# A float32 decoder layer on one Trainium2 core: branch products ahead of the gates, gate products by 2x2 blocks with seven products, merge through device memory

## The chip, the cores and the metric

The kernel runs on one core of a Trainium2 chip. A core has a matrix engine (TensorE, PE in the rows), two engines for element-wise work (VectorE, DVE, and ScalarE, ACT), a third one (GpSimd, POOL), and queues for transfers between device memory and the on-chip memory, issued here from SyncE (SP), ACT and POOL. Each engine works off its own instructions in the order of the program and waits by semaphores for the others. The metric is the time of one launch on the device in microseconds (us); lower is better.

## The reference

One decoder layer over x of 512 tokens by 2048 features, in float32:

```
proj = x @ W_in        # HGRN2 [q|f|i|g], attention [q|k|v], gates [gate_A|gate_B]
y_A  = hgrn2(q, f, i, g) @ W_A          # 1024 x 2048
y_B  = window_attention(q, k, v) @ W_B  # 1024 x 2048
x    = LN(alpha*x + (sigmoid(gate_A)*y_A + sigmoid(gate_B)*y_B) @ W_out)
x    = LN(alpha*x + relu(x @ W1)**2 @ W2)   # W1 2048 x 8192
```

What the change concerns is the middle: the two gates, each a product of x (512 x 2048) with 2048 columns of W_in, the two branch products y_A and y_B, and their sum weighted by the gates.

## The kernel before

Matrices lie on chip with features on the 128 partitions and the 512 tokens along the free dimension. Float32 precision is made from three products in a rounded 32-bit format: every operand is split into a high part (`hi`, made by ACT, line 84) and a low part (`lo = src - hi`, made by DVE, line 85), and `mm3` (lines 113 to 116) issues hi·hi, hi·lo and lo·hi for each pair. So each weight tile of 128x1024 costs a transfer on the SP queue, one ACT and one DVE instruction, and feeds 24 matmuls of 128x512 (moving size 512) or 24 of 128x256.

The stages run one after the other: attention, then HGRN2 by pairs of heads (`hg_pair`), then gates and branches, then `@ W_out` with the first LN, then the first product of the feed-forward part (FFN-1), its second product (FFN-2) and the second LN. The last thing each HGRN2 head does is `hg_out` (lines 480 to 508): a chain PE (L483, state updates) to DVE (L486, L488) to PE (L493, L495, the head's output) to ACT (L499, squares) to DVE (L500 to L502, an inverse square root by Newton steps and a product) to PE (L506, transposes) to DVE (L508). All its PSUM tiles come from the one bank `sc`, so two heads' chains go one after the other.

Gates and branches (lines 551 to 582) run over c = 0..7, 256 columns each: gate B (96 matmuls of 128x512), sigmoid on ACT, gate A (96), sigmoid, branch y_B (48), product with the gate on DVE, branch y_A (48), product on DVE and sum on POOL into `mix`, which stays on chip. At the end `mix` is split into `bh`, `bl`, the operands of `@ W_out`. The operands of the branches, `ath`, `atl` (from attention) and `oh`, `ol` (from HGRN2), are split at c = 0.

FFN-1 (lines 700 to 822) has 32 groups of 256 columns. The first four are plain (`head`: 96 matmuls of 128x512 a group). The other 28 cut the group's product into 2x2 blocks (two halves of the 2048 features, two halves of the 256 columns, two halves of the 512 tokens) and make it with seven block products in place of eight: each is 24 matmuls of 128x256 (`prod1`), and the sums of blocks that it needs are made on DVE, of the weights in each group (`tt`, 128x1024) and of x once ahead of the groups (`room`, `xq`: q6, q7 and q3, and q5 overwritten). In a group, product A takes the weights of block b11 as loaded, B needs the DVE sums, C a difference. Part of group g (`tail`: two products) is done inside group g+1.

The kernel is laid out by a scheduler that simulates the time of each instruction and sets each engine's order from it; what stands earlier in the program has the better priority. Buffers of weights: `raw` 3, `wh` 3, `wl` 2; `mz` 4 of 128x2048; PSUM `mm` 4 banks, `tp` 3, `sc` 1.

Of the kernel before, what the change touches and what calls it, by code (L numbers as in the profile page):

```python
# [10 lines left out]
F32 = mybir.dt.float32  # L11
F32R = mybir.dt.float32r
# [5 lines left out]
P = 128  # L18
# [34 lines left out]
def layer(ctx, tc, xt, xn, win, wa, wb, wo1, wo2, w1, w2, cst, vec, lnv, out):  # L53
# [56 lines left out]
    def wview(w, c):  # L110
        return w[0][:].rearrange("p (k c) -> p k c", c=c), w[1][:].rearrange("p (k c) -> p k c", c=c)
# [432 lines left out]
    pr_ctx = ExitStack()  # L544
    pb = pr_ctx.enter_context(tc.tile_pool(name="pb", bufs=1))
    ath = pb.tile([P, 8, T], F32R, name="ath")
    atl = pb.tile([P, 8, T], F32R, name="atl")
    oh = pb.tile([P, 8, T], F32R, name="oh")
    ol = pb.tile([P, 8, T], F32R, name="ol")
    mix = []  # L550
    for c in range(8):
        pgb = proj_fm([win[G_GB + c, q] for q in range(4)], bh, bl)
        sb = []
        for m in range(2):
            s = pb.tile([P, T], F32, tag="sb", bufs=2, name=nm("sb"))
            ACT.activation(s[:], pgb[m][:], AF.Sigmoid)
            sb.append(s)
        pga = proj_fm([win[G_GA + c, q] for q in range(4)], bh, bl)
        sa = []
        for m in range(2):  # L560
            s = pb.tile([P, T], F32, tag="sa", bufs=2, name=nm("sa"))
            ACT.activation(s[:], pga[m][:], AF.Sigmoid)
            sa.append(s)
        if c == 0:
            for i in range(8):
                split(ath[:, i, :], atl[:, i, :], att[i // 4][:, i % 4, :])
        yb = proj_fm([wb[c, q] for q in range(2)], ath, atl)
        if c == 0:
            for i in range(8):
                split(oh[:, i, :], ol[:, i, :], oT[i // 4][:, i % 4, :])  # L570
        if c % 2 == 0:
            mt = pm.tile([P, 4, T], F32, tag="mz", bufs=4, name=nm("mix"))
            mix.append(mt)
        ms = [mt[:, (c % 2) * 2 + m, :] for m in range(2)]
        for m in range(2):
            DVE.tensor_tensor(ms[m], yb[m][:], sb[m][:], op=ALU.mult)
        ya = proj_fm([wa[c, q] for q in range(2)], oh, ol)
        for m in range(2):
# [4 lines left out]
    pr_ctx.close()  # L583
# [3 lines left out]
    pf = fctx.enter_context(tc.tile_pool(name="pf", bufs=1))  # L587
    zs = []
# [94 lines left out]
    def keep(g, r):  # L683
        nc.gpsimd.dma_start(out=hd[g][:], in_=r)

    def head(g, o, part):

        ts = slice(0, T) if part is None else slice(part * CG, (part + 1) * CG)
        for kh in range(2):
            for m in range(2):  # L690
                wh, wl = wview(wload(w1[g, 2 * kh + m]), P)
                for k in range(8):
                    kc = kh * 8 + k
                    mm3(o[m][:, ts], wh[:, k, :], wl[:, k, :], bh[:, kc, ts], bl[:, kc, ts],
                        part != 1 and kc == 0, part != 0 and kc == KC - 1)

    def result():
        return pf.tile([P, 2, T], F32, tag="r", bufs=2, name=nm("r"))
# [3 lines left out]
    for part in range(2):  # L702
        for g in range(2):
            if part == 0:
                og[g] = [ps("mm"), ps("mm")]
            head(g, og[g], part)
    for g in range(NHEAD):
        if g not in og:
            og[g] = [ps("mm"), ps("mm")]
            head(g, og[g], None)  # L710
        r = result()
        for m in range(2):
            ACT.activation(r[:, m, :], og[g][m][:], AF.Relu)
        ACT.activation(r[:], r[:], AF.Square)
        keep(g, r[:].rearrange("p n t -> p (n t)"))

    count = [0]

    def wsplit(src):

        i = count[0] % 4
        count[0] += 1
        h, l = ("wh", "wh", "wh", "raw")[i], ("wl", "wl", "raw", "raw")[i]
        room = {"raw": 3, "wh": 3, "wl": 2}  # L730
# [19 lines left out]
    def tt(dst, a, b, op):  # L750
        DVE.tensor_tensor(dst, a, b, op=op)

    for u in range(2):
        k = slice(4 * u, 4 * u + 4)
        r0, r1, r2, r3 = (room[:, i, :].rearrange("p (k c) -> p k c", k=4) for i in range(4))

        def whole(r, q):
            tt(r, xo[q][0][:, k, :].bitcast(F32), xo[q][1][:, k, :].bitcast(F32), ALU.add)

        def put(q, src):  # L760
            split(xo[q][0][:, k, :], xo[q][1][:, k, :], src)

        whole(r0, "q1")
        whole(r1, "q5")
        tt(r2, r0, r1, ALU.subtract)
        put("q7", r2)
        whole(r3, "q4")
        tt(r3, r1, r3, ALU.add)
        tt(r0, r3, r0, ALU.subtract)
        put("q6", r0)  # L770
        whole(r1, "q2")
        tt(r1, r1, r0, ALU.subtract)
        put("q3", r1)
        put("q5", r3)

    def tmp(tag, bufs):
        return pf.tile([P, CG], F32, tag=tag, bufs=bufs, name=nm(tag))[:]

    def prod1(o, q, src, first, last):
        wh, wl = wview(wsplit(src), P)  # L780
        for k in range(8):
            mm3(o[:, :CG], wh[:, k, :], wl[:, k, :], xo[q][0][:, k, :], xo[q][1][:, k, :],
                first and k == 0, last and k == 7)

    def tail(g, B, C, U2, U3, E, t4, b22, R):
        prod1(B, "q4", t4, False, True)
        tt(R[:, 0, CG:], B[:, :CG], E, ALU.add)
        prod1(C, "q3", b22, False, True)
        tt(R[:, 1, :CG], C[:, :CG], U2, ALU.add)
        ACT.activation(R[:], R[:], AF.Relu)  # L790
        ACT.activation(R[:], R[:], AF.Square)
        keep(g, R[:].rearrange("p n t -> p (n t)"))

    left = None
    for g in range(NHEAD, NG):
        A, B, C = ps("mm"), ps("mm"), ps("tp")
        R = result()
        E, U2, U3 = tmp("E", 2), tmp("U2", 2), tmp("U3", 1)
        w = pair()
        b11, b12 = load(w[:, 0, :], w1[g, 0]), load(w[:, 1, :], w1[g, 1])  # L800
        prod1(A, "q1", b11, True, False)
        ACT.activation(E, A[:, :CG], AF.Copy)
        w = pair()
        b22, b21 = load(w[:, 0, :], w1[g, 3]), load(w[:, 1, :], w1[g, 2])
        tt(b11, b12, b11, ALU.subtract)
        t2_ = room[:, g % 2, :]
        tt(t2_, b22, b11, ALU.subtract)
        prod1(B, "q6", t2_, True, False)
        tt(U2, B[:, :CG], E, ALU.add)
        if left is not None:  # L810
            tail(*left)
        prod1(C, "q5", b11, True, False)
        prod1(A, "q2", b21, False, True)
        ACT.activation(R[:, 0, :CG], A[:, :CG], AF.Copy)
        tt(b12, b22, b12, ALU.subtract)
        prod1(B, "q7", b12, False, False)
        tt(U3, B[:, :CG], E, ALU.add)
        tt(R[:, 1, CG:], C[:, :CG], U3, ALU.add)
        tt(t2_, b21, t2_, ALU.subtract)
        left = (g, B, C, U2, U3, E, t2_, b22, R)  # L820
    tail(*left)
# [123 lines left out]

# [37 lines left out]
```

## Time and profile before

| | us |
|---|---|
| median of 3 runs | 2698.52 |
| lowest, highest | 2697.38, 2698.64 |
| the profiled execution | 2697.93 |
| its span in the trace | 2696.1 |
| PE busy | 2662.0 (99%) |
| DVE busy | 1479.9 (55%) |
| ACT busy | 1094.4 (41%) |
| POOL busy | 177.2 (7%) |

The span is from the first to the last instruction of the trace; the execution's own time holds 1.8 us around it. Busy time of PE counts pipelined matmuls that overlap, so a matmul's own duration (0.39 us for 128x512) is longer than the distance from one to the next. In the rows, "idle" and "<-" tell how long an engine stood before an instruction and what it waited for. The granted clock (PEclk) is the share of TensorE's full clock, 1.00 for 2.4 GHz and 0.50 for 1.2 GHz.

### The profile page before, as it was taken

The numbers are of one execution on the slowest core, as the hardware profiler recorded it, in microseconds if no ns is written. First come the engines' busy times: TensorE is split into PE (matmuls) and PEld (weight loads), VectorE is DVE, ScalarE is ACT, GpSimd is POOL, SyncE is SP. The second block draws the span as 40 slices with busy tenths as digits, with TensorE's granted clock in tenths as the row PEclk, the third lists the DMA queues.
The fourth block names the chain that finished last, engine by engine and source line by source line (L and its number), as shares of the span: only waits on it lengthen the run. The fifth ranks groups of instructions, "written<-read, shape, count | busy, mean of one in ns | idle before, by whom it ended". The sixth has DMA issues, their size and how long they took to land.

```text
span 2696.1 us, 37095 instructions
## 1 busy us (share of the span) xinstructions
PE 2662.0 (99%) x15264; PEld 2341.7 (87%) x15264; DVE 1479.9 (55%) x1953; ACT 1094.4 (41%) x1507; POOL 177.2 (7%) x152
## 2 busy tenths in 40 slices
PE   8999999999999999999999999999999999999998
PEld 8889788988888888888989999999988888888886
DVE  4588785664222222423868777777754454433346
ACT  4576655353222222312544444444443333322231
POOL 0110322120000000000200000000000000000001
PEclk9999999999999999999999999999999999999999
DMA  5322222222333333443543333333366555444442
GB/s 187 94 71 79 77 59 85 78 73 81 104 95 97 98 94 95 148 143 101 192 158 117 125 135 133 128 131 133 132 243 221 198 191 194 165 147 151 151 174 80
DMA packets 96362, 347.75 MB, mean 129 GB/s; under 512 B 10816, under 2 KB 11584, under 8 KB 94656
## 3 DMA queue, kind: packets, MB, share of 16 engines
q1 hardware_dynamic: 86976, 309.72, 35.4%
q0 software_dynamic: 5760, 25.17, 2.4%
q10 hardware_dynamic: 3456, 10.49, 1.1%
q8 instruction: 120, 1.97, 0.3%
q14 instruction: 50, 0.41, 0.0%
HBM read 320.16 MB, written 25.17 MB: 128 GB/s over the span
## 4 chain that ended last, share of the span: by engine, by line
PE 94%; DVE 4%; ACT 1%; DMA 1%; issue 0%; POOL 0%; SPq 0%; DVEq 0%; ACTq 0%
PE mm L116 23%; PE mm L115 23%; PE mm L114 23%; PE tp L114 6%; PE tp L116 6%; PE tp L115 6%; PE sc L116 1%; PE sc L114 1%; PE sc L115 1%; PE tp L444 1%; DVE wl L85 1%; PE tp L285 0%; PE tp L277 0%; DMA raw<-w 0%; DMA raw<-win 0%
## 5 line engine op out<-in xcount | busy, mean ns | idle before, releaser
L114 PE MATMUL mm<-bh,wh 128*128 128x512 f32 (+1 forms) x1920 | 664.0, 346 | 2.1 <-ACT wh L84 1.5
L116 PE MATMUL mm<-bh,wl 128*128 128x512 f32 (+1 forms) x1920 | 663.0, 346 | 1.6 <-DVE wl L85 1.6
L115 PE MATMUL mm<-bl,wh 128*128 128x512 f32 (+1 forms) x1920 | 664.1, 346 | 0.0
L85 DVE TENSOR_TENSOR wl<-raw,wh 128x1024 fp32r<-128x1024 f32 (+1 forms) x239 | 295.4, 1236 | 490.8 <-PE mm L116 311.5
L84 ACT ACTIVATE wh<-raw 128x1024 fp32r<-128x1024 f32 (+1 forms) x239 | 250.4, 1048 | 549.9 <-PE mm L115 393.1
L85 DVE TENSOR_TENSOR wl<-raws,wh 128x1024 fp32r<-128x1024 f32 x262 | 320.1, 1223 | 224.7 <-ACT wh L84 224.5
L84 ACT ACTIVATE wh<-raws 128x1024 fp32r<-128x1024 f32 x262 | 276.2, 1055 | 393.6 <-PE mm L115 241.8
L114 PEld LDWEIGHTS mm<-bh,wh 128*128 128x128 f32 x1920 | 363.8, 190 | 45.6 <-ACT wh L84 1.9
L116 PEld LDWEIGHTS mm<-bh,wl 128*128 128x128 f32 x1920 | 363.6, 189 | 45.5 <-DVE wl L85 2.6
L115 PEld LDWEIGHTS mm<-bl,wh 128*128 128x128 f32 x1920 | 363.8, 190 | 42.7
L85 DVE TENSOR_TENSOR hl<-raws,hh 128x1024 fp32r<-128x1024 f32 x94 | 114.8, 1224 | 228.5 <-ACT hh L84 228.4
L84 ACT ACTIVATE hh<-raws 128x1024 fp32r<-128x1024 f32 x94 | 99.1, 1058 | 260.2 <-PE mm L115 255.0
L114 PE MATMUL mm<-wh,hh 128*128 128x512 f32 x472 | 183.6, 389 | 0.0
L115 PE MATMUL mm<-wl,hh 128*128 128x512 f32 x472 | 183.6, 389 | 0.0
L116 PE MATMUL mm<-wh,hl 128*128 128x512 f32 x472 | 183.6, 389 | 0.0
L114 PE MATMUL mm<-wh,bh 128*128 128x256 f32 (+1 forms) x448 | 138.8, 312 | 6.2 <-ACT bh L84 5.6
L115 PE MATMUL mm<-wl,bh 128*128 128x256 f32 (+1 forms) x448 | 138.0, 309 | 0.8 <-DVE wl L85 0.8
L114 PE MATMUL tp<-wh,hh 128*128 128x512 f32 x356 | 138.5, 389 | 0.0
L115 PE MATMUL tp<-wl,hh 128*128 128x512 f32 x356 | 138.5, 389 | 0.0
L116 PE MATMUL tp<-wh,hl 128*128 128x512 f32 x356 | 138.5, 389 | 0.0
L116 PE MATMUL mm<-wh,bl 128*128 128x256 f32 (+1 forms) x448 | 137.4, 308 | 0.0
L114 PE MATMUL mm<-xq,wh 128*128 128x256 f32 x448 | 126.9, 283 | 1.4 <-ACT wh L84 1.4
(325 smaller groups left out, 4784.1 us busy)
## 6 DMA issues: line engine op xcount, KB each, us to landing
raws<-w SPq DMA_DIRECT2D x240, 512.0 KB, 4.5
raw<-win SPq DMA_DIRECT2D x151, 512.0 KB, 3.6
raws<-hd SPq DMA_DIRECT2D x96, 512.0 KB, 3.6
raw<-wo SPq DMA_DIRECT2D x32, 512.0 KB, 3.6
hd<-r POOLq DMA_DIRECT2D x32, 512.0 KB, 3.0
raw<-w SPq DMA_DIRECT2D x24, 512.0 KB, 4.2
raw<-wb SPq DMA_DIRECT2D x16, 512.0 KB, 3.5
raw<-wa SPq DMA_DIRECT2D x16, 512.0 KB, 3.6
```

The source lines that it names most:

```text
L84: ACT.activation(hi, src, AF.Copy)
L85: DVE.tensor_tensor(lo, src, hi.bitcast(F32), op=ALU.subtract)
L114: PE.matmul(o, ah, bh_, start=first, stop=False, skip_group_check=True)
L115: PE.matmul(o, ah, bl_, start=False, stop=False, skip_group_check=True)
L116: PE.matmul(o, al, bh_, start=False, stop=last, skip_group_check=True)
L444: PE.matmul(pl[:, c * P:(c + 1) * P], qk[:, c * P:(c + 1) * P], qk[:, c * P:(c + 1) * P], start=True, stop=True)
```

## The change

The gate columns of W_in go to an input of their own, `wg`, on the host: 16 groups of 256 columns, gate B and gate A of each c in turn, in the block layout of W1. FFN-1's code (`plain`, `operands`, `Sevens` with `group` and `rest`) is moved ahead and made into functions and a class, with the same work; it now serves gates and FFN-1. In place of the loop over c the kernel runs

- all eight c of y_B, then all eight of y_A; each result is copied from PSUM by ACT (L695) into a tile `r` and written to device memory (`yd`) by a transfer on the POOL queue;
- gate groups 0 and 1 plainly, as before;
- the block sums of x (`operands`, L590 and L85), placed with group 1, in tile `room`;
- groups 2 to 15 by `Sevens`;
- for every group `merge`: the branch result is loaded on the ACT queue into slot 2 or 3 of `room` (L704), sigmoid on ACT (L705), product on DVE (L590), and a write to device memory (`md`) on the POOL queue, for gate A a write that adds (L708);
- at the end `md` is loaded on the SP queue and split into `bh`, `bl`.

In the diff `...` marks what is left out; the bodies of `plain`, `wsplit`, `prod1`, `group` and `rest` are those of `head`, `wsplit`, `prod1`, the loop over g and `tail` of before.

```
-    for c in range(8):
-        pgb = proj_fm([win[G_GB + c, q] for q in range(4)], bh, bl)
-        sb = []
-        for m in range(2):
...
-            ACT.activation(s[:], pgb[m][:], AF.Sigmoid)
...
-        pga = proj_fm([win[G_GA + c, q] for q in range(4)], bh, bl)
...
-        yb = proj_fm([wb[c, q] for q in range(2)], ath, atl)
...
-            DVE.tensor_tensor(ms[m], yb[m][:], sb[m][:], op=ALU.mult)
-        ya = proj_fm([wa[c, q] for q in range(2)], oh, ol)
-        for m in range(2):
-            DVE.tensor_tensor(sa[m][:], ya[m][:], sa[m][:], op=ALU.mult)
-            POOL.tensor_tensor(ms[m], ms[m], sa[m][:], op=ALU.add)
-    for i in range(KC):
-        split(bh[:, i, :], bl[:, i, :], mix[i // 4][:, i % 4, :])
...
+    def wide():
+        return pf.tile([P, 4, 1024], F32, tag="h", bufs=4, name=nm("room"))
...
+    yd = [[pd.tile([P, 1024], F32, name=f"yd{i}_{c}") for c in range(8)] for i in range(2)]
+    md = [pd.tile([P, 1024], F32, name=f"md{c}") for c in range(8)]
+
+    def half():
+        return pf.tile([P, 8, T], F32R, tag="h", bufs=4, name=nm("half"))
+
+    for i, (w, y) in enumerate(((wb, att), (wa, oT))):
+        yh, yl = half(), half()
+        for k in range(8):
+            split(yh[:, k, :], yl[:, k, :], y[k // 4][:, k % 4, :])
+        for c in range(8):
+            o = proj_fm([w[c, q] for q in range(2)], yh, yl)
+            r = result()
+            for m in range(2):
+                ACT.activation(r[:, m, :], o[m][:], AF.Copy)
+            nc.gpsimd.dma_start(out=yd[i][c][:], in_=flat(r))
+
+    room = wide()
+
+    def merge(g, R):
+        y = room[:, 2 + g % 2, :]
+        nc.scalar.dma_start(out=y, in_=yd[g % 2][g // 2][:])
+        ACT.activation(R[:], R[:], AF.Sigmoid)
+        tt(flat(R), flat(R), y, ALU.mult)
+        if g % 2:
+            nc.gpsimd.dma_start(out=md[g // 2][:], in_=flat(R), accum_op=ALU.add)
+        else:
+            nc.gpsimd.dma_start(out=md[g // 2][:], in_=flat(R))
+
+    NPLAIN = 2
+    for g in range(NPLAIN):
+        o = [ps("mm"), ps("mm")]
+        plain(wg[g], o, None)
+        R = result()
+        for m in range(2):
+            ACT.activation(R[:, m, :], o[m][:], AF.Copy)
+        if g == NPLAIN - 1:
+            xo = operands(room)
+        merge(g, R)
+    sevens = Sevens(xo, room, merge)
+    for g in range(NPLAIN, 16):
+        sevens.group(g, wg[g])
+    sevens.rest()
+    for c in range(8):
+        if c % 2 == 0:
+            raw = pair()
+        m = load(raw[:, c % 2, :], md[c][:])
+        split(bh[:, 2 * c:2 * c + 2, :].rearrange("p k t -> p (k t)"),
+              bl[:, 2 * c:2 * c + 2, :].rearrange("p k t -> p (k t)"), m)
```

**The order at the end of HGRN2.** PE, from the last head pair's state updates on, before. `sc_5808` is the first of the two heads' chains, `mm_5907` and `mm_5908` are the PSUM tiles of gate B at c = 0:

```order
L114 MATMUL mm_5907<-bh,wh_5910 128x512
L483 MATMUL sc_5808<-v_5805,kT_5461 128x128 x3
L115 MATMUL mm_5907<-bl,wh_5910 128x512
L116 MATMUL mm_5907<-bh,wl_5911 128x512
L114 MATMUL mm_5908<-bh,wh_5910 128x512
L115 MATMUL mm_5908<-bl,wh_5910 128x512
L116 MATMUL mm_5908<-bh,wl_5911 128x512
L114 MATMUL mm_5907<-bh,wh_5940 128x512
```

And now, with the whole of both heads' chains; `mm_5945` and the three after it are PSUM tiles of the first two column groups of y_B:

```order
L116 MATMUL mm_5588<-wh_5752,bl 128x256
L483 MATMUL sc_5808<-v_5805,kT_5461 128x128 x3
L493 MATMUL sc_5816<-v_5805,SB_2016 128x128 x2
...
L506 MATMUL sc_5847<-ident,on_5825 128x128 x4
L483 MATMUL sc_5853<-v_5805,kT_5585 128x128 x3
L493 MATMUL sc_5861<-v_5805,SB_2017 128x128 x2
...
L506 MATMUL sc_5892<-ident,on_5870 128x128 x4
L114 MATMUL mm_5945<-half_5927,wh_5948 128x512
L114 MATMUL mm_5946<-half_5927,wh_5948 128x512
L114 MATMUL mm_6011<-half_5927,wh_6014 128x512
L114 MATMUL mm_6012<-half_5927,wh_6014 128x512
```

The gate matmuls that stood between the steps of the two chains (23 ahead of `sc_5816`'s first in the order of before) are gone from there; nothing stands between them now, and the tiles `half`, which the first branch matmuls read, are split after the last step of the second chain.

**The order ahead of the first block products.** DVE, before, at the start of FFN-1's block groups. `wl_11280` holds low parts for product A, `wl_11314` those for product B, `raws` are loaded weights:

```order
L85 TENSOR_TENSOR wl_11200<-raw_11198,wh_11199 128x1024
L751 TENSOR_TENSOR room<-room 128x1024 x2
L751 TENSOR_TENSOR room<-bh,bl 128x1024
L85 TENSOR_TENSOR bl<-room,bh 128x4x256
L85 TENSOR_TENSOR wl_11280<-raws_11276,wh_11279 128x1024
L85 TENSOR_TENSOR xq_1546_11234<-room,xq_1546_11234 128x1024
L751 TENSOR_TENSOR room<-room 128x1024
L751 TENSOR_TENSOR raws_11276<-raws_11276 128x1024
L85 TENSOR_TENSOR xq_1548_11236<-room,xq_1548_11236 128x1024
L751 TENSOR_TENSOR room<-raws_11308,raws_11276 128x1024
L751 TENSOR_TENSOR raws_11276<-raws_11308,raws_11276 128x1024
L85 TENSOR_TENSOR wl_11314<-room,wh_11313 128x1024
```

And now, ahead of the gates' block groups, where `r_7142` is the result of plain group 0, `r_7271` that of group 1, `wl_7213` and `wl_7243` the last weights of plain group 1, `wl_7324` product A's and `wl_7358` product B's of group 2; from the first row here to the last there are 29 instructions:

```order
L590 TENSOR_TENSOR r_7142<-r_7142,room_7019 128x1024
L590 TENSOR_TENSOR room_7019<-room_7019 128x1024 x2
L590 TENSOR_TENSOR room_7019<-bh,bl 128x1024
L85 TENSOR_TENSOR wl_7213<-raw_7211,wh_7212 128x1024
...
L85 TENSOR_TENSOR wl_7324<-raws_7320,wh_7323 128x1024
...
L590 TENSOR_TENSOR room_7019<-raws_7352,raws_7320 128x1024
L590 TENSOR_TENSOR r_7271<-r_7271,room_7019 128x1024
L85 TENSOR_TENSOR xq_1122_7276<-room_7019,xq_1122_7276 128x1024
L85 TENSOR_TENSOR wl_7358<-room_7019,wh_7357 128x1024
```

The block sums of x stand in one piece between the merge of group 0 and the weights of product B, and the merges of groups 0 and 1 stand among them; before, the same sums were spread over the plain groups and only a few were left behind `wl_11200`.

## Rows read from the trace of the kernel before

**Rows 1.** The page: busy time and instructions by engine.
```profile
PE 2662.0 (99%) x15264; PEld 2341.7 (87%) x15264; DVE 1479.9 (55%) x1953; ACT 1094.4 (41%) x1507; POOL 177.2 (7%) x152
```
**Rows 2.** Windows, gates then block groups: length, busy (x instructions) by engine, clock, DMA.
```profile
664.00:1138.30 474.30, 474.30 (x2094) 392.86 (x2093) 146.50 (x142) 119.87 (x139) 24.68 (x14) 1.00 0.34 104
1460.00:1943.84 483.84, 483.84 (x4034) 483.84 (x4033) 361.99 (x385) 236.53 (x265) 12.76 (x24) 1.00 0.39 131
```
**Rows 3.** Waits from 1460 to 1940 us: total, times, longest.
```profile
POOL hd L684 <- ACT r L791: 471.1, 24, 19.6
```
**Rows 4.** Timeline of PE: end of HGRN2, and the first matmul of W_out.
```profile
609.48 0.40 PE L114 MATMUL mm<-bh,wh 128*128 128x512 f32 x1
...
613.82 0.83 PE L483 MATMUL sc<-v,kT 128*128 128x128 f32 x6
...
632.00 0.60 PE L506 MATMUL sc<-ident,on 128*128 128x128 f32 x4
...
644.07 0.60 PE L493 MATMUL sc<-v,SB 128*128 128x128 f32 x4
...
1139.21 0.39 PE L114 MATMUL sc<-wh,bh 128*128 128x512 f32 x1
```
**Rows 5.** Timelines of ACT and DVE: steps of the two heads' chains at HGRN2's end.
```profile
608.96 1.32 ACT L533 ACTIVATE v<-mm 128x512 f32<-128x512 f32 x2 [4.30 <-PE mm L116]
645.83 0.28 ACT L499 ACTIVATE on<-sc 128x128 f32<-128x128 f32 x1 [4.59 <-PE sc L495]
...
615.01 0.73 DVE L488 SCALAR_TENSOR_TENSOR state<-state,ebl,sc 128x128 f32<-128x128 f32 x2
...
624.09 0.16 DVE L500 TENSOR_SCALAR ss<-ss 128x4 f32<-128x4 f32 x1
...
626.47 0.69 DVE L502 TENSOR_TENSOR on<-sc,y 128x512 f32<-128x512 f32 x1
...
632.64 0.75 DVE L508 SCALAR_TENSOR_TENSOR oT<-sc,vecs,oT 128x512 f32<-128x512 f32 x1 [3.01 <-PE sc L506]
...
647.00 0.17 DVE L500 TENSOR_SCALAR ss<-ss 128x4 f32<-128x4 f32 x1 [5.32 <-ACT on L499]
```
**Rows 6.** Timelines of DVE and ACT: block sums of FFN-1, and a table load with sigmoids.
```profile
1414.71 1.22 DVE L85 TENSOR_TENSOR wl<-raws,wh 128x1024 fp32r<-128x1024 f32 x1
1415.85 1.22 DVE L85 TENSOR_TENSOR xq<-room,xq 128x1024 fp32r<-128x1024 f32 x1
...
656.76 1.28 ACT L556 ACT_TABLE_LOAD   x1 [3.03 <-PE sc L506]
658.05 1.09 ACT L556 ACTIVATE sb<-mm 128x512 f32<-128x512 f32 x2
```
**Rows 7.** Timeline of PE at the start of FFN-1's block groups.
```profile
1421.58 0.28 PE L116 MATMUL mm<-bh,wl 128*128 128x256 f32 x1
1423.28 0.39 PE L114 MATMUL mm<-xq,wh 128*128 128x256 f32 x1 [1.42 <-ACT wh L84]
```
**Rows 8.** The page: transfers, KB each and us from issue to landing.
```profile
raws<-zd ACTq DMA_DIRECT2D x4, 512.0 KB, 4.6
z<-zd ACTq DMA_DIRECT2D x8, 256.0 KB, 11.3
```
**Rows 9.** Windows around PE's last matmul (columns as in rows 2).
```profile
2683.00:2684.00 1.00, 0.11 (x1) 0.00 (x0) 0.82 (x2) 0.00 (x0) 0.00 (x0) 1.00 0.36 129
...
2686.00:2687.00 1.00, 0.00 (x0) 0.00 (x0) 0.96 (x2) 1.00 (x2) 0.97 (x1) 0.50 0.00 0
```
**Rows 10.** Timeline of PE in the kernel's first 11 us.
```profile
5.58 0.58 PE L114 MATMUL mm<-wh,bh 128*128 128x256 f32 x1 [5.58 <-ACT bh L84]
...
6.39 0.41 PE L115 MATMUL mm<-wl,bh 128*128 128x256 f32 x1
6.60 0.41 PE L116 MATMUL mm<-wh,bl 128*128 128x256 f32 x1
...
10.03 0.28 PE L114 MATMUL mm<-wh,bh 128*128 128x256 f32 x1
```
**Rows 11.** Window in HGRN2 in which PE waits (columns as in rows 2).
```profile
340.00:350.00 10.00, 7.29 (x53) 6.32 (x52) 7.55 (x17) 8.13 (x19) 5.34 (x5) 1.00 0.19 52
```

More of the change, by code (lines that the diff above doesn't have):

```diff
@@ new lines, in pair, with load, tt, operands @@
+    def pair():
+        return pm.tile([P, 2, 1024], F32, tag="mz", bufs=4, name=nm("raws"))
+    def load(dst, src):
+        nc.sync.dma_start(out=dst, in_=src)
+        return dst
+    def tt(dst, a, b, op):
+        DVE.tensor_tensor(dst, a, b, op=op)
+    def wide():
+        return pf.tile([P, 4, 1024], F32, tag="h", bufs=4, name=nm("room"))
+    def operands(room):
+        xo = {"q1": (bh[:, 0:8, 0:CG], bl[:, 0:8, 0:CG]), "q2": (bh[:, 8:16, 0:CG], bl[:, 8:16, 0:CG]),
+              "q5": (bh[:, 0:8, CG:T], bl[:, 0:8, CG:T]), "q4": (bh[:, 8:16, CG:T], bl[:, 8:16, CG:T])}
+        for q in ("q6", "q7", "q3"):
+            t_ = pf.tile([P, 2, 8, CG], F32R, tag="h", bufs=4, name=nm("x" + q))
+            xo[q] = (t_[:, 0], t_[:, 1])
+        for u in range(2):
+            k = slice(4 * u, 4 * u + 4)
+            r0, r1, r2, r3 = (room[:, i, :].rearrange("p (k c) -> p k c", k=4) for i in range(4))
+            def whole(r, q):
+                tt(r, xo[q][0][:, k, :].bitcast(F32), xo[q][1][:, k, :].bitcast(F32), ALU.add)
+            def put(q, src):
+                split(xo[q][0][:, k, :], xo[q][1][:, k, :], src)
+            whole(r0, "q1")
+            whole(r1, "q5")
+            tt(r2, r0, r1, ALU.subtract)
+            put("q7", r2)
+            whole(r3, "q4")
+            tt(r3, r1, r3, ALU.add)
+            tt(r0, r3, r0, ALU.subtract)
+            put("q6", r0)
+            whole(r1, "q2")
+            tt(r1, r1, r0, ALU.subtract)
+            put("q3", r1)
+            put("q5", r3)
+        return xo
@@ L683, in keep, with relu @@
     def keep(g, r):
[L684 to L698, printed above, removed]
+        ACT.activation(r[:], r[:], AF.Square)
+        nc.gpsimd.dma_start(out=hd[g][:], in_=flat(r))
+    def relu(g, r):
+        ACT.activation(r[:], r[:], AF.Relu)
+        keep(g, r)
     og = {}
@@ L705, in layer @@
                 og[g] = [ps("mm"), ps("mm")]
[L706 removed]
+            plain(w1[g], og[g], part)
     for g in range(NHEAD):
@@ L709, in layer @@
             og[g] = [ps("mm"), ps("mm")]
-            head(g, og[g], None)
+            plain(w1[g], og[g], None)
         r = result()
@@ L750, in tt @@
[L750 to L792, printed above, removed]
@@ L794, in layer @@
-    left = None
-    for g in range(NHEAD, NG):
[L796 to L820, printed above, removed]
@@ L821, in layer @@
-    tail(*left)
+        keep(g, r)
+    room = wide()
+    sevens = Sevens(operands(room), room, relu)
+    for g in range(NHEAD, NG):
+        sevens.group(g, w1[g])
+    sevens.rest()
     fctx.close()
```

131 lines of the change are left out of this document (78 added, 53 removed).

## The prediction

> **What bounds the kernel now.** I read the page first. PE is busy for 2662 of 2696 us [rows 1], so time can only come from fewer or shorter matmuls, and every microsecond in which PE stands is added to the end. Then the windows, one stage each, for the distance between matmuls, which is what a stage costs: in the gate stage 474.30 us for 2094 matmuls of 128x512, 0.2265 us each; in FFN-1's block groups 483.84 us for 4034 of 128x256, 0.120 us each [rows 2]. Half the columns cost 53% of the time. PE has no idle time in either window, while DVE works for 31% of the first and 75% of the second. So the block form runs at PE's pace in FFN-1; 168 matmuls at 0.120 are 20.16 us a group, and POOL, which writes each group's result, waits 471.1/24 = 19.6 us from one write to the next [rows 3]. Then the timelines at the two places where PE's work is fed by a chain: the end of HGRN2 [rows 4, 5] and the start of the block groups [rows 6, 7]. The question for the change is whether it keeps PE fed there.
>
> **The sums are made against the profiled execution, 2697.93 us; the median of the runs is 0.6 us above it.**
>
> **Fewer matmuls.** A plain gate group is 96 matmuls of 0.2265 = 21.74 us, a block group 7 x 24 = 168 of 0.120 = 20.16 us: 1.58 us less, for 14 groups **-22.2 us**. One product in eight is saved, 12.5%, and 7.3% is left of it, since a half-wide matmul is not half as long. By the Trainium skill (TensorE: Matmul & The Clock Gate, section Back-to-back issue gap) an isolated matmul of N columns takes N/2.4 + 2.5 ns, so the sum here would be an estimated -33 us in place of -22; the trace has 0.120 where that gives 0.109, and the trace decides. The 32 column groups of branches (768 matmuls of 128x512) are the same before and after.
>
> **The end of HGRN2.** Before, gate B's matmuls stood between the steps of the last two heads' chains. They cost nothing there: from the first gate matmul at 609.48 to W_out's first at 1139.21 are 529.73 us [rows 4], 2304 matmuls of 0.2265 are 521.8, and 7.9 are left for the chains' own matmuls and all else. Now nothing stands between, so PE goes at the chain's pace. One head, from rows of steps of either head [rows 4, 5]: state matmuls and update 613.82 to 615.74, 1.9; the output's matmuls 644.07 to 645.83, 1.8; squares 645.83 to 647.00, 1.2; Newton steps and product 624.09 to 627.16, 3.1; transposes 632.00 to 632.64, 0.6; last product 0.75. That is 9.3, and with some 0.1 for the handovers that lie between the rows of different heads 9.5. Both heads use the one bank `sc`, so two chains are 19.0. Ahead of them V's copy ends at 610.28, 0.8 after the last projection; behind them the first split of `half` (hi and lo) costs about 0.7. In all 20.5. PE does four branch matmuls in it (0.9) and no longer has the 7.9: 20.5 - 7.9 - 0.9 = **+11.7 us**. Could the scheduler have put the splits and y_B ahead? y_B needs attention alone, but its operands come from a pool that opens where HGRN2's closes, and the order shows them behind the last chain.
>
> **The start of the block groups.** The block sums write slot 2 of `room`, which holds y_B for the merge of group 0 until its product on DVE; so they begin behind it. That product needs group 0's results copied (1.1), a table load (1.28) and the sigmoid of both halves (1.09 for two of half the size) [rows 6]: it starts about 4 us after PE begins plain group 1, with its handovers. From there to `wl_7358`, the low weights of product B, DVE has 29 instructions, all of 128x1024, at 1.14 apart [rows 6]: 33 us. One of them, the merge of group 1, waits for y_A in slot 3, whose load is issued only when q5 has been split from that slot, about 30 us in, and takes 4.6 as the like transfer on ACT's queue does [rows 8]: 1.5 us more. `wl_7358` is ready 38.5 us after group 1 began. PE meanwhile has group 1 (21.7) and product A (2.9): done at 24.6; of what comes next, four matmuls can go ahead (0.5). It stands for **+13.4 us**. At FFN-1's start, where the sums were spread over four plain groups, PE stood for 1.42 at one place [rows 7]. These are the bounds: 1.4 if the sums here get done as early as there, and 20 if y_A's load takes 11.3 instead of 4.6 [rows 8]. I take the count of instructions, since the order puts all 29 in a row, in a queue that can't pass them.
>
> **The clock.** After the kernel's last matmul, which ends in the window from 2683 to 2684, the granted clock is 0.50 in the window from 2686 [rows 9]; the kernel's first matmuls go 0.21 us apart (6.39 to 6.60), at half pace, from 5.58 until about 10.0 [rows 10], which costs about half of these 4.4 us, 2.2. Both new gaps are far longer than 3 us, so I expect 1.2 GHz in them and some 2.1 us for each restart. The chains' own matmuls at half pace add about 1. **+5 us.** The bounds are 0 (it stays at 2.4 GHz) and 7 (the last chains' step times grow by more). Gaps in HGRN2's middle, 2.7 us in all within 10, left it at 1.00 [rows 11]; a gap as long as these is not in the trace but at the two ends of the kernel. By the Trainium skill (same page, section HAM oscillation) waits between groups of matmuls put the engine back to half rate each time anew; no run shown here has one inside the kernel.
>
> **The rest.** A block group gets one DVE product (1.14) and its wait for y: DVE goes from 75% of 20.16 us to 81%, below PE. Its sigmoid takes the place of Relu and Square. y, `md` and the weights together add 1 to 1.5 MB per 20.16 us, some 50 to 75 GB/s on top of 131 [rows 2]; weights are asked for a group ahead. `md` for the last column block is needed by W_out some 38 us after its start (24 matmuls for each of seven earlier weight tiles), so a write, an adding write and a load hide there; an adding write is not in the trace, and its cover is those 38 us. If that cover were gone, it would be three transfers one after another, some 14 us by the 4.6 of rows 8. FFN-1 is the same work in a slightly other order; 0. Copies of branch results on ACT and their writes have 10.9 us a group; 0.
>
> **Sum:** -22.2 + 11.7 + 13.4 + 5 = **+7.9**, so 2705.8 for a profiled execution and **2706.5** beside the median of 2698.52.
>
> **Rivals.**
> (1) The block sums are out of the way in time, and PE waits 1.4 as in FFN-1: then there is no second fall of the clock either. -22.2 + 11.7 + 1.4 + 3 = -6.1, **2692**, faster. It decides where PE first waits for product B's low weights: below about 2 us of wait the change wins by more than 5. For it: FFN-1 does just that [rows 7]. Against it: the order, 29 instructions in one queue behind a merge.
> (2) The clock does not fall in the gaps, or the few small matmuls hold it up: -22.2 + 11.7 + 13.4 = +2.9, **2701.5**, no change that could be told. For it: 1.00 with PE at 73% in HGRN2 [rows 11]. Against it: rows 9.
> (3) The merge binds the block groups: DVE at 81%, and ACT, which has to issue y's load behind a slot that DVE still reads, would hold the next split back. At the product's 1.14 to 1.25 for each of 14 groups that is +16 to +17: **2723**, slower. Against it: 20% of DVE's time is free.
> (4) The block groups' matmuls go closer together than FFN-1's, as by the page's formula: each nanosecond of the 2352 is 2.4 us, so 5 ns give **2695**. Against it: 4034 matmuls without a wait at 0.120 [rows 2].
>
> **Chances.** The forecast, with gaps and a fall of the clock: 0.60; of it 0.05 come out within 0.2% because the two gaps are each a few us shorter. Rival 1: 0.12, faster. Rival 2: 0.14, within 0.2%. Rival 3: 0.10, slower. Rival 4: 0.04, within 0.2%. 0.2% is 5.4 us, about what a measurement can tell here. So faster 0.12, within 0.2% 0.05 + 0.14 + 0.04 = 0.23, slower 0.55 + 0.10 = 0.65. The range, 2696 to 2718, takes in rival 2 and the bounds of the second gap (half of the way to its lower one, 6 us more at its upper one) and of the clock (5 less, 2 more); rivals 1 and 3 are left out, 0.2 in all.
>
> **What would show it.** Right: one stretch of about 20 us from 610 on with only the chains' small matmuls, its granted clock at 0.50; then 768 branch matmuls; a gap of 12 to 14 us between about 853 and 866 that ends with a split of weights by DVE (L85, `wl` from `room`), again at 0.50; after it 20.16 us from group to group and no gap ahead of W_out. Wrong: PE at work through the second place (rival 1), a clock of 1.00 in both (rival 2), groups longer than 20.3 us with PE waiting for DVE or ACT in each (rival 3). If W_out's first products wait for `md`, the cover of the last merge is shorter than I think. What would overturn it most cheaply is the DVE chain: at 20 instructions instead of 29 ahead of `wl_7358`, the gap would be 3 us.

## The result, and the profile after

| | before | changed |
|---|---|---|
| median (6 runs each) | 2698.58 | 2713.52 |
| lowest, highest | 2697.38, 2698.77 | 2710.63, 2716.36 |
| the profiled execution, its span | 2697.93, 2696.1 | 2713.84, 2712.1 |

The ratio is 1.0056, with a 95% interval of 1.0043 to 1.0069: slower, by 14.9 us, inside the range and 7.0 us above the forecast. Three matmuls that both programs have, read from the timelines of PE, show where the 16.0 us between the two spans lie:

| stretch | before | changed | difference | forecast |
|---|---|---|---|---|
| start to the last matmul of HGRN2's last projection | 609.36 | 611.98 | +2.6 | 0 |
| from there to W_out's first matmul | 529.85 | 542.19 | +12.3 | +7.9 |
| from there to the end of the span | 1556.9 | 1557.9 | +1.0 | 0 |

The page of the changed kernel, busy time by engine, answers to [rows 1]: PE has 1008 matmuls more and 9 us less of busy time, in a span that is 16 us longer.

```profile
PE 2652.9 (98%) x16272; PEld 2382.2 (88%) x16272; DVE 1637.7 (60%) x2121; ACT 1168.3 (43%) x1597; POOL 169.3 (6%) x168
```

Its waits of PE (in all, times, longest) name both places of the forecast: one wait of 10.2 us for a split of weights, two of 4.4 us for the output of a head, and four for a head's state, of which two (1.15 us each) lie at the end of HGRN2; the other two, in its middle, the kernel before has as well.

```profile
PE mm L114 <- ACT wh L84: 14.2, 6, 10.2
PE sc L506 <- DVE on L502: 8.9, 2, 4.4
...
PE sc L493 <- DVE state L488: 5.3, 4, 1.7
```

**The end of HGRN2.** PE's timeline of the changed kernel, where [rows 4] had gate matmuls between the steps:

```profile
612.24 1.20 PE L483 MATMUL sc<-v,kT 128*128 128x128 f32 x6
614.59 0.71 PE L493 MATMUL sc<-v,SB 128*128 128x128 f32 x4 [1.15 <-DVE state L488]
...
620.85 1.09 PE L506 MATMUL sc<-ident,on 128*128 128x128 f32 x4 [4.43 <-DVE on L502]
622.77 1.65 PE L483 MATMUL sc<-v,kT 128*128 128x128 f32 x6 [0.84 <-DVE oT L508]
625.58 1.23 PE L493 MATMUL sc<-v,SB 128*128 128x128 f32 x4 [1.15 <-DVE state L488]
...
633.37 1.09 PE L506 MATMUL sc<-ident,on 128*128 128x128 f32 x4 [4.44 <-DVE on L502]
635.27 2.05 PE L114 MATMUL mm<-half,wh 128*128 128x512 f32 x4 [0.81 <-issue]
```

The six state matmuls took 1.20 us in the first chain and 1.65 in the second; the output's first four went from 0.71 to 1.23, and all of the output's matmuls (up to ACT's squares) from 1.9 to 3.4; the transposes took 1.09 in both, 0.60 in the kernel before. The windows (columns as in rows 2, the granted clock is third from the end) say why: it fell while PE waited for the first chain's output, and came back nearly 6 us after branch matmuls had begun. The 1.20 of the first chain, 0.83 before, is not the clock, which was 1.00 there: the last two of the six waited for V's second copy.

```profile
618.00:620.00 2.00, 0.00 (x0) 0.00 (x0) 1.66 (x12) 0.00 (x0) 0.00 (x0) 1.00 0.00 0
620.00:622.00 2.00, 1.09 (x4) 0.71 (x4) 0.72 (x2) 0.00 (x0) 0.00 (x0) 0.65 0.00 0
622.00:624.00 2.00, 1.23 (x5) 1.23 (x6) 0.72 (x1) 0.00 (x0) 0.00 (x0) 0.50 0.00 0
...
638.00:640.00 2.00, 2.00 (x6) 1.62 (x5) 2.00 (x4) 2.00 (x5) 0.00 (x0) 0.50 0.62 195
640.00:642.00 2.00, 2.00 (x8) 1.54 (x8) 2.00 (x5) 2.00 (x5) 0.00 (x0) 0.73 1.02 406
```

From the last projection to plain group 0 (812.17) are 200.2 us; 768 branch matmuls of 0.2265 are 174.0. So 26.2 us are lost here: 23.0 in the two chains (612.24 to 635.25), 2.8 in branch matmuls at half pace, 0.4 around them. Before, 7.9 were lost in the whole stage: +18.3.

**The start of the block groups.** PE's timeline: product A's last matmul, product B's first, the first with B's low weights, and one of the first at full pace again:

```profile
858.46 0.28 PE L116 MATMUL mm<-bh,wl 128*128 128x256 f32 x1
868.98 0.58 PE L114 MATMUL mm<-xq,wh 128*128 128x256 f32 x1 [10.24 <-ACT wh L84]
...
872.12 0.58 PE L116 MATMUL mm<-xq,wl 128*128 128x256 f32 x1 [1.40 <-DVE wl L85]
...
876.56 0.30 PE L115 MATMUL mm<-xq,wh 128*128 128x256 f32 x1
```

And DVE's, first and last of the 29 instructions with the merge of group 1, which alone waited behind the first; where [rows 7] had PE waiting 1.42 us:

```profile
837.85 1.23 DVE L590 TENSOR_TENSOR r<-r,room 128x1024 f32<-128x1024 f32 x1 [2.44 <-ACT r L705]
...
868.57 1.22 DVE L590 TENSOR_TENSOR r<-r,room 128x1024 f32<-128x1024 f32 x1 [0.73 <-DMA room<-yd]
...
870.85 1.22 DVE L85 TENSOR_TENSOR wl<-room,wh 128x1024 fp32r<-128x1024 f32 x1
```

From 858.58 to 872.12 PE did four matmuls: 13.1 us lost. The 20 matmuls after it went 0.213 us apart instead of 0.120, another 1.9, at a granted clock of 0.50 (the windows of 864 and 874; it fell while PE stood):

```profile
860.00:862.00 2.00, 0.00 (x0) 0.00 (x0) 2.00 (x3) 1.16 (x2) 0.00 (x0) 1.00 0.00 0
...
864.00:866.00 2.00, 0.00 (x0) 0.00 (x0) 2.00 (x3) 0.00 (x0) 0.00 (x0) 0.50 0.83 264
...
874.00:876.00 2.00, 2.00 (x11) 2.00 (x11) 2.00 (x3) 0.00 (x0) 0.00 (x0) 0.50 0.96 162
```

**The block groups with their merge.** POOL's timeline has one write of `md` a group, 20.16 us apart as in [rows 2], and the window over the groups has PE idle for 0.9 of 274 us and DVE busy for 80%:

```profile
920.73 0.86 POOL L708 DMA_DIRECT2D md<-r  x1 [19.61 <-DVE r L590]
940.88 0.55 POOL L710 DMA_DIRECT2D md<-r  x1 [19.29 <-DVE r L590]
961.05 0.87 POOL L708 DMA_DIRECT2D md<-r  x1 [19.62 <-DVE r L590]
```

```profile
880.00:1154.00 274.00, 273.11 (x2276) 272.93 (x2276) 218.47 (x232) 122.33 (x139) 10.14 (x15) 1.00 0.53 167
```

18.3 + 13.1 + 1.9 - 22.2 are 11.1 of the 12.3 us of the stage. Of the other 1.2, 0.9 are one wait inside the block groups (PE's idle time in the window); 0.3 are not placed.

### The profile page after: what moved, and what is told of

Read it like the earlier page. It is cut to its first block, busy times and chain, and to the rows that moved or that the text cites. A ratio compares the mean times of both kernels' runs of the same rounds, so it can differ in the third digit from the quotient of the medians.

```text
span 2712.1 us, 39517 instructions
## 1 busy us (share of the span) xinstructions
PE 2652.9 (98%) x16272; PEld 2382.2 (88%) x16272; DVE 1637.7 (60%) x2121; ACT 1168.3 (43%) x1597; POOL 169.3 (6%) x168
## 4 chain that ended last, share of the span: by engine, by line
PE 92%; DVE 5%; ACT 1%; DMA 1%; issue 1%; POOL 0%; DVEq 0%; SPq 0%; ACTq 0%
PE mm L114 21%; PE mm L116 21%; PE mm L115 21%; PE tp L116 7%; PE tp L114 7%; PE tp L115 7%; PE sc L115 1%; PE sc L114 1%; PE sc L116 1%; DVE wl L85 1%; PE tp L444 1%; DVE room L590 1%; DMA raw<-w 1%; PE tp L285 0%; PE tp L277 0%
## 5 line engine op out<-in xcount | busy, mean ns | idle before, releaser
L114 PE MATMUL mm<-bh,wh 128*128 128x256 f32 (+1 forms) x1808 | 585.6, 324 | 3.9 <-ACT wh L84 2.4
L116 PE MATMUL mm<-bh,wl 128*128 128x256 f32 (+1 forms) x1808 | 585.0, 324 | 0.5 <-DVE wl L85 0.4
L115 PE MATMUL mm<-bl,wh 128*128 128x256 f32 (+1 forms) x1808 | 585.4, 324 | 0.0
L84 ACT ACTIVATE wh<-raws 128x1024 fp32r<-128x1024 f32 x332 | 350.2, 1056 | 493.0 <-PE mm L115 319.6
L85 DVE TENSOR_TENSOR wl<-raws,wh 128x1024 fp32r<-128x1024 f32 x332 | 404.8, 1223 | 239.0 <-ACT wh L84 238.4
L85 DVE TENSOR_TENSOR wl<-raw,wh 128x1024 fp32r<-128x1024 f32 (+1 forms) x183 | 221.4, 1210 | 343.3 <-PE mm L116 193.2
L84 ACT ACTIVATE wh<-raw 128x1024 fp32r<-128x1024 f32 (+1 forms) x183 | 190.9, 1044 | 303.9 <-PE mm L115 153.4
L85 DVE TENSOR_TENSOR hl<-raws,hh 128x1024 fp32r<-128x1024 f32 x94 | 114.8, 1224 | 235.3 <-ACT hh L84 235.1
L114 PE MATMUL mm<-xq,wh 128*128 128x256 f32 x672 | 191.6, 285 | 10.8 <-ACT wh L84 10.2
L116 PE MATMUL mm<-xq,wl 128*128 128x256 f32 x672 | 191.3, 285 | 1.5 <-DVE wl L85 1.4
L115 PE MATMUL mm<-xq,wh 128*128 128x256 f32 x672 | 191.1, 284 | 0.0
L114 PEld LDWEIGHTS mm<-xq,wh 128*128 128x128 f32 x672 | 130.1, 194 | 11.2 <-ACT wh L84 10.4
```

The lines of the kernel that those rows point to most:

```text
L114: PE.matmul(o, ah, bh_, start=first, stop=False, skip_group_check=True)
L115: PE.matmul(o, ah, bl_, start=False, stop=False, skip_group_check=True)
L116: PE.matmul(o, al, bh_, start=False, stop=last, skip_group_check=True)
```

## The experiments

Each is set beside runs of the kernel before on its own chip, whose medians there were 2699.6 (e1 to e4), 2700.5 (e5 to e8) and 2700.3 (e9, e10). The edits of e1_tail to e5_plain are shown against the changed kernel, those of the later runs against the run that they build on; `...` marks what is left out. "Stage" is the stretch from HGRN2's last projection to W_out's first matmul: 529.9 us before, 542.2 in the changed kernel.

**e1_tail: plain gate groups back between the chains.**

```
+    for g in range(2):
+        R = result()
+        gate(g, R, "tp" if g else "mm")      # plain, as before
+        ACT.activation(R[:], R[:], AF.Sigmoid)
+        nc.gpsimd.dma_start(out=gd[g][:], in_=flat(R))
     for i, (w, y) in enumerate(((wb, att), (wa, oT))):
...
-    NPLAIN = 2
+    NPLAIN = 4      # groups 0 and 1: gd loaded and merged; 2 and 3 plain
...
```

> Two plain gate groups (g = 0, 1) stand ahead of the branch products again, between the steps of the last two HGRN2 chains as in the kernel before; their sigmoids go to device memory and are merged later. Groups 2 and 3 are then the plain ones behind the branches, so 12 groups go by seven products instead of 14 (+3.2 us). Theory (the bare chains cost time, clock included): in the changed kernel 26.1 us stand between the last projection of HGRN2 and a steady stream of branch matmuls beyond the matmuls' own time, in the kernel before 7.9; so 18.2 less, plus 3.2: about 2698.5, and the gap of 13 us ahead of the first block products stays. Rival (the time is lost elsewhere, the chains' time would come back as a wait of the branches for their operands): 2710 to 2716, with PE waiting for ACT or DVE where the branches begin.

Measured: 2706.92 (1.0026, 1.0015 to 1.0036). The stage took 531.9, 10.3 less; PE was at work in all of the 47 us in which the chains now lie (the window), and the branches began behind waits of 0.2 and 1.1 us. The gap ahead of product B stayed (9.4 us for the high, 1.7 for the low weights). What the forecast missed is a new wait at W_out's start; without its 5.8 us the stage would be 16.1 shorter, 15.0 were expected. W_out's stage behind that wait is 2.3 longer, with its first matmuls at half pace, so the two make up 8.1 of the 8.4 us by which the time misses 2698.5.

```profile
612.00:659.00 47.00, 47.00 (x233) 39.49 (x231) 17.30 (x43) 11.29 (x27) 0.00 (x0) 1.00 0.28 90
```

```profile
659.54 0.70 PE L114 MATMUL mm<-half,wh 128*128 128x512 f32 x2 [0.22 <-issue]
...
1141.80 0.79 PE L114 MATMUL sc<-wh,bh 128*128 128x512 f32 x1 [5.77 <-ACT wh L84]
```

So the bare chains were the loss, and the rival falls: of their time only those 1.3 us came back as a wait of the branches. Why W_out waits was open until e9_turn.

**e2_slots: branch results of groups 0 and 1 in a tile of their own.**

```
+    ys = []
...
-        y = room[:, 2 + g % 2, :]
+        if g < 2:
+            if g % 2 == 0:
+                ys.append(pair())
+            y = ys[g // 2][:, g % 2, :]
+        else:
+            y = room[:, 2 + g % 2, :]
```

> Only the place of the branch results for groups 0 and 1 changes: they are loaded into a tile of their own instead of slots 2 and 3 of room, so the block sums of x need not wait for the merge of group 0 and begin while y_A is still being made. From the merge of group 0 on 18 instead of 29 DVE instructions are left ahead of product B's low weights. Theory (the gap is the DVE chain behind the merge): PE waits 0 to 3 us there instead of 13, the clock stays at 2.4 GHz there (2 us more): about 2699, 2697 to 2702. Rival (product B waits for something else, its weights' transfer or ACT): a gap of about 13 stays, 2711 to 2715.

Measured: 2703.53 (1.0015, 1.0006 to 1.0024), 10 below the changed kernel; the stage 530.3, 11.9 less. PE's waits ahead of product B shrank to three short ones:

```profile
858.52 0.39 PE L114 MATMUL mm<-xq,wh 128*128 128x256 f32 x1 [1.42 <-ACT wh L84]
859.47 0.39 PE L114 MATMUL tp<-bh,wh 128*128 128x256 f32 x1 [0.45 <-ACT wh L84]
860.61 0.58 PE L116 MATMUL mm<-xq,wl 128*128 128x256 f32 x1 [0.64 <-DVE wl L85]
860.99 0.41 PE L114 MATMUL mm<-xq,wh 128*128 128x256 f32 x1
```

The gap was the DVE chain behind the merge: from the start of plain group 0 to B's low weights 50.1 us instead of 60.0. But the matmuls behind these waits go 0.21 apart: the clock fell after waits of 2.5 us in all. That is some 2 of the 4.5 us by which the time misses 2699; FFN-1's stage, which the edit does not touch, is 1.5 longer; the last us is not placed.

**e4_fill: the gap filled with matmuls whose result nobody reads (idle matmuls).**

```
+        return wh      # at the end of prod1
...
-            prod1(A, xo["q1"], b11, True, False)
+            wa_ = prod1(A, xo["q1"], b11, True, False)
+            if g == 2:
+                f = ps("sc")
+                for i in range(100):
+                    PE.matmul(f[:, :CG], wa_[:, i % 8, :], bh[:, i % 8, 0:CG], start=True, stop=True)
```

> 100 matmuls of 128x256 whose result nobody reads are put behind product A's first weights, so that PE works through most of the gap ahead of product B; all else is as in the changed kernel. They need 12.0 us where PE stands for 13.5. Theory (the gap lowers the granted clock, and the restart at 1.2 GHz costs about 2 us): the gap's end stays where it is, the granted clock stays at 1.00 behind it, product B's matmuls go 0.12 us apart from the first on, and the time is 1.5 to 2 us below the changed kernel, about 2711.5. Rival (the slow matmuls behind the gap have another cause, such as the weights' arrival): product B's first twenty matmuls go 0.21 us apart again, and the time is that of the changed kernel or above it.

Measured: 2712.85 (1.0048, 1.0036 to 1.0061); from B's low weights to W_out 280.1 us instead of 282.05, 2.0 less. The gap's end stayed: from plain group 0 to B's low weights 60.2 us, in the changed kernel 60.0. The distance is 0.12 from the second matmul on, where the changed kernel had 0.21:

```profile
870.84 0.39 PE L116 MATMUL mm<-xq,wl 128*128 128x256 f32 x1 [1.19 <-DVE wl L85]
871.06 0.28 PE L114 MATMUL mm<-xq,wh 128*128 128x256 f32 x1
871.18 0.28 PE L115 MATMUL mm<-xq,wh 128*128 128x256 f32 x1
```

So the restart behind this gap costs 2 us, and idle matmuls in it held the clock (1.00 in every window from 858 to 874). The medians alone, 0.7 apart on two chips, would not have told it.

**e5_plain: the order and the merge alone.**

```
-    NPLAIN = 2
+    NPLAIN = 16     # no block sums, no Sevens for the gates
...
```

> The new order and the merge through device memory alone: all 16 gate groups plain, no block sums, no block products. Theory: the chains at HGRN2's end stand bare (26 us lost there instead of 8), nothing waits ahead of product B because there is none, and plain groups with their merge run at 21.74 us as before: 18 us above the kernel before, so about 2717 (2714 to 2720), a few us above the changed kernel, since its block products save 22 and give back about 15 at their start. Rival (the merge through device memory costs time of its own in each group): groups longer than 21.9 us and a time above 2722.

Measured: 2717.66 (1.0064, 1.0051 to 1.0078), as expected. From plain group 0 on PE has no wait:

```profile
810.95:1154.00 343.05, 343.05 (x1515) 284.10 (x1514) 100.43 (x83) 103.68 (x116) 11.00 (x16) 1.00 0.53 157
```

So the merge through device memory costs nothing in plain groups (1515 matmuls at 0.2264), and the order costs all, 17.2 us against the kernel before. By the profiles, from the last projection to FFN-1's first matmul it is 709.4 us in the kernel before, 727.9 here and 722.1 in the changed kernel: fourteen block groups leave a gain of 5.8 us, of 22. Their start takes 15.0 of the rest, the wait inside them 0.9. By the medians, which hold the rest of the program too, the gain is 2 to 4 us.

**e3_both: e1_tail and e2_slots together.**

```
+    EARLY = 2                 # as e1_tail
...
-    NPLAIN = 2
+    NPLAIN = 4
...
-        y = room[:, 2 + g % 2, :]
+        if g < 4:                 # as e2_slots, for four groups
...
```

> e1_tail and e2_slots together: plain groups 0 and 1 ahead of the branches, 2 and 3 behind them, twelve groups by seven products, branch results of the first four groups in tiles of their own. Theory: both losses go, 18.2 + 15 less 3.2: about 2684, faster than the kernel before by 14 to 15 us, which is 12 groups of 1.58 us less the few us that are left at the two places. Rival (the savings overlap, or the block groups with their merge give less than 1.58 us each): 2690 to 2699.

Measured: 2698.16 (0.9992, 0.9983 to 1.0001), no difference to the kernel before; 14 us short of the theory. The profile is of an execution of 2694.36 us, the lowest of the eleven times, so what it shows covers only a part of the 14. In it the stage is 520.2, 22.0 less than in the changed kernel, where 30 were expected. The 8 that are missing are the wait at W_out's start (3.6) and the start of product B, where 3.2 are lost in waits and some 1.5 in matmuls at half pace. W_out's and FFN-1's stages are 4.4 us longer than in the changed kernel, though the edit is not there; 1.7 of that are in W_out's stage, behind its wait.

**e6_pool: `md` loaded on POOL's queue.**

```
-        m = load(raw[:, c % 2, :], md[c][:])
+        m = raw[:, c % 2, :]
+        nc.gpsimd.dma_start(out=m, in_=md[c][:])
```

> e3_both with the eight loads of the merged gates (md) issued on POOL's queue, behind the writes that they read, instead of on SP's queue. In e3_both PE waited 3.6 us for W_out's first weights, whose load stood on SP's queue behind md loads that waited for their data for 13 us. Theory: that wait goes and W_out's stage is shorter: 3 to 6 us below e3_both's 2698.2, about 2693.5. Rival (W_out's weights are late for want of a buffer, or W_out then waits for md itself): a wait of 3 us or more stays at W_out's start, 2697 to 2700.

Measured: 2699.40 (0.9996, 0.9987 to 1.0005), no difference to the kernel before. The theory falls: with `md` off SP's queue PE waited longer, 6.68 us, and W_out's first load was issued at 1125.61, 9.5 before the matmul. The row names a split of weights, not `md`; whether the load came late for want of a buffer, as the rival has it, e9_turn shows.

```profile
1135.14 0.80 PE L114 MATMUL sc<-wh,bh 128*128 128x512 f32 x1 [6.68 <-ACT wh L84]
```

```profile
1125.61 11.09 SPq L92 DMA_DIRECT2D raw<-wo  x4
```

**e9_turn: the buffers' rotation.** `wsplit` takes (wh, wl) twice, then (wh, raw), then (raw, raw), by a count.

```
+    count[0] = 2
     sevens = Sevens(xo, room, merge)          # of the gates
...
+    count[0] = 0
     sevens = Sevens(operands(room), room, relu)   # of FFN-1
```

> e6_pool with the rotation of the split weights' buffers begun two steps on at the gates (and set back ahead of FFN-1): every fourth product takes its two tiles from the raw buffers into which weights are loaded. With twelve groups (84 products) the last product of the gates is such a one, and W_out's first load waits for a raw buffer; two steps on it is not. Theory (the wait of 4 to 7 us at W_out's start in e1_tail, e3_both, e6_pool and e8_hold, and its absence in the changed kernel and e7_three, is this rotation): the wait goes, and with it the fall of the clock behind it: 7 to 10 us below e6_pool, about 2691. Rival (W_out's first weights land late because the loads of md and of x compete with them): a wait of 3 us or more stays, 2697 to 2700.

Measured: 2687.28 (0.9956, 0.9944 to 0.9969), 12.1 below e6_pool. PE has no wait at W_out's start; its first load is issued at 1117.37, 9.6 us ahead of the matmul at 1126.93:

```profile
1117.37 9.71 SPq L92 DMA_DIRECT2D raw<-wo  x4
```

The stage is 513.6, 9.7 less than e6_pool's, and W_out up to FFN-1's first matmul 179.6 instead of 181.9. Of the 9.7, 6.7 are the wait; the rest lies at the start of the block groups, where the new rotation leaves waits of 0.52 and 0.44 us (1.42, 0.45 and 0.65 in e6_pool) and the clock at 1.00. So it was the rotation: a product that takes two of the three tiles into which weights are loaded, as the last before the next stage. ACT's split of the first such tile of W_out began 7.0 us after the issue here (1124.41) and 8.4 in e6_pool (1134.03), so an issue just ahead of its use shows as a wait. What makes these loads that slow was not tried.

**e7_three: one plain group behind the branches.**

```
-        if g < 4:
+        if g < 3:
...
-    NPLAIN = 4
+    NPLAIN = 3
```

> e6_pool with one plain group behind the branches instead of two, so 13 groups by seven products (1.6 us less). Theory (the plain groups are the cover of the block sums): the sums that need the tiles which y_A's operands leave only at the end of the branches, some 26 DVE instructions, take 30 us, PE has 24.6 us of work: it stands 5 to 8 us ahead of product B, the clock falls there, and the time is 5 to 8 us above e6_pool. Rival (one group is cover enough): 1 to 2 us below e6_pool.

Measured: 2688.20 (0.9956, 0.9943 to 0.9968), 11.2 below e6_pool where the theory had 5 to 8 above. PE did stand, as the theory says, longer ahead of product B (from plain group 2 to B's low weights 31.1 us where its matmuls need 25.1: 6.0, against 3.2):

```profile
866.60 0.48 PE L114 MATMUL mm<-xq,wh 128*128 128x256 f32 x1 [4.75 <-ACT wh L84]
```

But with 13 groups (91 products) the rotation ends elsewhere, and W_out's wait of 6.7 is gone, with 2.3 behind it; from FFN-1's first matmul on it took 3.2 less. So PE's wait was as the theory has it, and the total was set by the buffers' rotation, which the theory left out.

**e8_hold and e10_best: idle matmuls in short waits.** e6_pool with ten of them at the two starts of block groups, and e7_three with forty and ten.

```
...
+            if self.n == 0:
+                f = ps("sc")
+                for i in range(10):        # e10_best: 40 in the gates, and NPLAIN = 3
+                    PE.matmul(f[:, :CG], wa_[:, i % 8, :], bh[:, i % 8, 0:CG], start=True, stop=True)
```

> e6_pool with ten matmuls of 128x256 whose result nobody reads behind product A's first weights, at the start of the gates' and of FFN-1's block groups, where PE waits 1.4 us and twice about 0.5. Theory (waits of 1 to 3 us in a row can already lower the granted clock for the next 4 us, at 2 us each time): the clock stays at 1.00 at both places, and the time is 1 to 4 us below e6_pool, with less spread. Rival (such short waits leave the clock alone): within 1 us of e6_pool.

Measured: 2694.72 (0.9981, 0.9973 to 0.9990), 4.7 below e6_pool: more than expected. The same 2 us of both profiles, behind product B's first weights, e6_pool:

```profile
888.00:890.00 2.00, 2.00 (x11) 2.00 (x11) 2.00 (x3) 0.00 (x0) 0.00 (x0) 0.50 0.86 279
```

and e8_hold:

```profile
888.00:890.00 2.00, 2.00 (x20) 2.00 (x18) 2.00 (x3) 0.76 (x1) 0.00 (x0) 1.00 0.96 309
```

From B's low weights to W_out it took 2.6 us less, of which 1.05 is a shorter wait at W_out's start, and FFN-1's stage 2.6 less, of which 1.0 are shorter waits in its plain groups: a fall of the clock costs some 1.5 us at either place, also behind waits of 1.9 to 2.5 us in all.

> e7_three (two plain gate groups ahead of the branches, one behind, thirteen groups by seven products, md loaded on POOL's queue) with matmuls whose result nobody reads in PE's waits at the start of the block groups: 40 of 128x256 in the gates, where it waits 6 us, ten in FFN-1. Theory (the clock falls behind the gates' wait and costs 2 us, while in FFN-1 it held in e7_three's profile): 1 to 3 us below e7_three's 2688.2, about 2686, 13 us below the kernel before. Rival: within 1 us of e7_three.

Measured: 2689.57 (0.9960, 0.9946 to 0.9973): not below e7_three. The gates' stage gained 1.0 us; FFN-1's start got a wait of 4.55 us that e7_three does not have, for weights, in rows that the edit does not touch (the scheduler laid out the rest anew). What set that wait was not tried.

```profile
1339.06 0.39 PE L114 MATMUL mm<-bh,wh 128*128 128x256 f32 x1 [4.55 <-ACT wh L84]
```

e9_turn and e7_three beat both kernels, by 12 to 13 us against the one before.

## Why the prediction held, and where it was off

- **Fewer matmuls, -22.2.** Right: 20.16 us from group to group, 2276 matmuls in 273.11 us, 0.120 each; rival 4 is out. The rule of the isolated matmul (the Trainium skill, TensorE: Matmul & The Clock Gate, section Back-to-back issue gap) would give an estimated 0.109; no hundred 128x256 matmuls in a row go closer than 0.120 in either trace.
- **The end of HGRN2, +11.7 and 3 for the clock.** The mechanism was right (e1_tail, e5_plain), the size was not: +18.3. The term that was mis-sized is the chain's length, 9.5 us a head from steps at full clock, with 1 us for the clock in both, 20.0 in all: the first took 10.5 (612.24 to 622.72; 0.4 of it is V's second copy, 0.5 the transposes at half clock), the second 12.5 (622.77 to 635.25), at 0.50, with 1.5 of the 2.0 between them in the output's matmuls. So the fall of the clock slowed not only the restart but every PE step of the second chain. The branch stream then went at half pace for nearly 6 us, which cost 2.8 where 2.1 were forecast. The forecast's 0.8 ahead of the chains and 0.7 behind them, less 0.9 for four branch matmuls, came to 0.4.
- **The start of the block groups, +13.4.** Right at 13.1, by the count: 29 instructions, the first begun at 837.85, the last at 870.85, 33.0 us. Its one wait, for y_A, was 0.73 instead of 1.5. e2_slots shows the cause.
- **The clock, restart of 2.1.** Right: 1.9 behind the gap; e4_fill takes it away. By the Trainium skill (same page, section HAM oscillation) waits between groups of matmuls put the engine back to half rate each time; the trace agrees at these two places, 0.50 from 622 to 640 and from 864 to 876. Shorter waits did not lower it each time (last section). Rival 2 is out.
- **The rest, 0.** Right for the merge: DVE at 80% (81 was forecast), one PE wait of 0.9 us in 274, none in e5_plain, W_out not waiting for `md`; rival 3 is out. The sum had nothing for short waits; they are 1.2 us in the stage. An adding write took 7.9 us to land (median of eight), in the cover that was named for it.
- **Not in the sum:** 2.6 us ahead of the stage, where the program is the same. PE waited 1.60 us at 15 us for early weights, 0.64 before, and its clock was then 0.50 from 17 to 19 us. In the twelve profiles of this study the last projection comes between 609.4 and 613.3, at 609.9 in e1_tail and e3_both, so this is spread, not the change. The 1.0 us behind W_out's first matmul is not placed.
- **Rival 1** (2692, the block sums out of the way) is out: PE stood for 10.24 and 1.40 us. e2_slots gets the sums out of the way and comes to 2703.5, since its short waits still lower the clock and the chains cost more than the sum has. Only with both places mended and the buffers in turn does e9_turn reach 2687.
- **The total.** The forecast has the sign and both places, and half of the size: +7.9, of a measured +14.9. The larger errors have one sign and did not cancel: the 3.5 us at the end of HGRN2 and the 3.6 outside the stage. A range of 22 us took them in.

## What to carry to other kernels

When matmuls are taken from between the steps of a serial chain, the chain's whole length can appear, as 23.0 us did here, and it grew once the clock fell; before moving such work, list what fills each chain now and what will. Operand preparation belongs where its buffers are free, and a tile shared between it and a result that is used first ties the two together. Where buffers go round by a count, look at which one the last user before the next stage holds: one group more moved the time by 11 us (e7_three against e6_pool), 9.0 of it at W_out for that reason.

## What the hardware showed that was not expected

Waits shorter than those at the kernel's ends were also followed by a lower clock, but not each time. In the kernel before, 1.42 and 0.44 us at FFN-1's block start [rows 7] left it at 1.00; in e6_pool the same waits, 1.42 and 0.45, were followed by 0.50 for about 3.5 us. Six profiles have this pair of waits there: the clock held in the kernel before and e5_plain and fell in e1_tail, e3_both, e6_pool and e9_turn. The window from 1424 on, of the kernel before:

```profile
1424.00:1426.00 2.00, 1.77 (x14) 1.76 (x15) 2.00 (x3) 2.00 (x3) 0.00 (x0) 1.00 0.00 0
```

and of e6_pool:

```profile
1424.00:1426.00 2.00, 2.00 (x12) 2.00 (x11) 2.00 (x3) 1.06 (x2) 0.00 (x0) 0.50 0.00 0
```

This may be part of why e6_pool's times spread over 6.6 us (11 runs) and those of e7_three, whose waits there were shorter (0.82 and 0.45) and left the clock at 1.00 in its profile, over 0.9 (5 runs); it is not shown. What decides whether the clock falls behind such waits was not found.
